# One chain of softmax steps for each chunk of a head pair, instead of one for the two chunks of a head pair

## The chip, the cores and the metric

The kernel runs on one core of a Trainium2 chip. The metric is the device time of one execution in microseconds, as the median of several runs. A profile of one execution goes with it. The engines are named as in the profile: PE is TensorE (PEld its weight loads), DVE is VectorE, ACT is ScalarE, POOL is GpSimd, and SP issues most of the transfers. Each engine works through its own queue in order and waits on semaphores where it needs another engine's result.

## The reference, cut to what matters

The kernel is one step of a hybrid decoder layer, for a prompt of 256 tokens and for 8 sample tokens together (264 columns). One combined input projection gives the operands of a sliding-window attention (16 heads of 64, 4 key heads, window 128, a learned sink per head) and of a state-space mixer; an output projection, a cross-attention and a convolutional feed-forward part follow. The change touches the prompt's sliding-window attention alone:

```python
qb = q.reshape(b, nb, WINDOW, N_KV_HEADS, Q_PER_KV, HEAD_DIM)      # nb = 2 chunks of 128 tokens
logits = jnp.einsum('bnqkgd,bnskd->bnkgqs', qb, kk) * HEAD_DIM ** -0.5
mask = ((diff >= 0) & (diff <= WINDOW))[None] & ((blk > 0) | (sj >= WINDOW)[None])
p = sink_softmax(logits, mask[None, :, None, None], sinks...)       # softmax over the keys and the sink
o = jnp.einsum('bnkgqs,bnskd->bnqkgd', p.astype(v.dtype), vv)
```

Chunk 0 has 128 keys (its own chunk), chunk 1 has 256 (both chunks). The query's RMS norm is not applied to the queries; its factor per row, `rq`, is the scale of the exponential.

## The kernel before, in words

All activations lie with features on the 128 partitions and tokens along the free axis. Weights come in tiles of 128 x 2048 on SP's queue (line 74); ScalarE rounds each half to `whi` (L86, some by VectorE) and VectorE takes the rest `wlo` (L87). Each product is three matmuls (L101 to L103). The input projection goes by pairs of output blocks, `in_pair` (L324): pair 0 gives the keys, pair 1 the values, pairs 2 to 5 the queries, 6 to 9 the B and C operands of the mixer, 10 to 17 its x (two pairs for each `conv_group`), 18 to 25 its gate z. A pair's two results are read out by VectorE at high priority, for the mixer into a ring of three `u` buffers, from which VectorE and ScalarE compute a convolution.

PSUM has eight banks, by tag: `mm` three, `t` two, and `s`, `x` and `y` one each (L58). The pairs write to `mm`, but pair 0 and the odd pairs above 13 write to `t` (L328), so pair 15 is the first behind the attention that needs both `t` banks.

The prompt's attention (`attn_prompt`, L401) runs after the queries' pairs in the text, once for each of eight pairs of heads j, with two chunks c of 128 queries:

1. logits of two heads by one matmul (L410), for chunk 0 into a `t` bank and for chunk 1 into the `s` bank;
2. VectorE adds the mask into a tile in SBUF (L411) and takes the row maxima (L412). The tile of chunk 0 has the tag `e0` (two buffers), that of chunk 1 the tag `h0` (three buffers). The profile calls both `pe`;
3. for both chunks together (128 x 4): times the negative factor `nrq` (L414), the minimum with the negative sink (L415), the sink added (L416), and one exponential for the sink (L417);
4. four exponentials with their row sums (L420); for both chunks together the sink's part added and the reciprocal (L422, L423); four scalings by it (L427);
5. for each chunk: transposes by PE into a `t` bank (L164), a copy to SBUF by ScalarE (L433, tile `pt`), weighted sums of the values by PE into another `t` bank (L437), and a copy to `attn` (L439).

So one head pair takes five `t` tiles: logits, then transposes and sums of chunk 0, then of chunk 1. The statistics tile `st` has four buffers. The sample's attention (`attn_sample`, L457) follows, with two `s` tiles, two `t` tiles (L490 and L497) and two `h0` tiles; the sample's part of the mixer (`ssd_sample`, L644) loads its state on POOL's queue (L651) into `h0` tiles as well.

The order on the engines is not the order of the text. A planner runs the whole program through a simulation at build time, with its own costs, and puts on each engine the earliest written instruction that is ready there (parts under `tc.high_priority()` first). The order that it finds is fixed in the program. Tiles of one tag take turns in its buffers, and what needs a buffer waits until the tile before has been read.

Of the kernel before, what the change touches and what calls it, by code (L numbers as in the profile page):

```python
# [7 lines left out]
F32 = mybir.dt.float32  # L8
F32R = mybir.dt.float32r
AF = mybir.ActivationFunctionType  # L10
ALU = mybir.AluOpType
AX = mybir.AxisListType
# [35 lines left out]
def hybrid_decoder_step_kernel(ctx: ExitStack, tc: tile.TileContext, I, O):  # L48
    nc = tc.nc
    V, S, P, PE = nc.vector, nc.scalar, nc.gpsimd, nc.tensor  # L50
# [9 lines left out]
    def psum(tag):  # L60
        return ps.tile([128, 512], F32, tag=tag, name=tag, bufs=banks[tag])
# [87 lines left out]
    def pc(name, i=0, n=1):  # L149
        o = _PC[name][0]  # L150
        return par[:, o + i:o + i + n]
# [6 lines left out]
    maskb = cst[:, C_MASK:C_MASK + 256]  # L158
# [3 lines left out]
    def tr(out, in_):  # L162
        k = in_.shape[0]
        PE.transpose(out, in_, cst[0:k, C_ID:C_ID + k])  # L164
# [56 lines left out]
    mp = mix.enter_context(tc.tile_pool(name="mp", bufs=1))  # L221
# [7 lines left out]
    p = psum("mm")  # L229
# [41 lines left out]
    p = psum("x")  # L271
# [5 lines left out]
    p = psum("x")  # L277
# [114 lines left out]
    p = psum("y")  # L392
# [5 lines left out]
    nsink = mp.tile([128, 16], F32, name="nsink")  # L398
    V.tensor_scalar(out=nsink, in0=pc("sink_p", 0, 16), scalar1=-1.0, scalar2=None, op0=ALU.mult)

    def attn_prompt(j, rq, nrq):  # L401
        pp = j // 4
        ps_ = [psum("t"), psum("s")]
        evs = [mp.tile([128, 2, 128], F32, tag="e0", name="pe0", bufs=2), mp.tile([128, 2, 256], F32, tag="h0", name="pe", bufs=3)]
        st = mp.tile([128, 3, 2, 2], F32, tag="st", name="st", bufs=4)
        mx, den, es = st[:, 0], st[:, 1], st[:, 2]
        for c in range(2):
            nk = 128 * (c + 1)
            s3 = ps_[c][:, 0:2 * nk].rearrange("p (h k) -> p h k", h=2)
            PE.matmul(s3, qT[:, j, c * 128:c * 128 + 128], kbd[:, pp, :, 0:nk], start=True, stop=True)  # L410
            V.tensor_tensor(out=evs[c], in0=s3, in1=maskb[:, 256 - nk:256].unsqueeze(1).broadcast_to([128, 2, nk]), op=ALU.add)  # L411
            V.tensor_reduce(out=mx[:, c, :], in_=evs[c], op=ALU.max, axis=AX.X)  # L412

        V.tensor_tensor(out=mx, in0=mx, in1=nrq, op=ALU.mult)  # L414
        V.tensor_tensor(out=mx, in0=mx, in1=nsink[:, 2 * j:2 * j + 2].unsqueeze(1).broadcast_to([128, 2, 2]), op=ALU.min)  # L415
        V.tensor_tensor(out=es, in0=mx, in1=pc("sink_p", 2 * j, 2).unsqueeze(1).broadcast_to([128, 2, 2]), op=ALU.add)  # L416
        S.activation(out=es, in_=es, func=AF.Exp)  # L417
        for c in range(2):
            for h in range(2):
                S.activation(out=evs[c][:, h, :], in_=evs[c][:, h, :], func=AF.Exp, scale=rq[:, c, h:h + 1], bias=mx[:, c, h:h + 1],  # L420
                             accum_out=den[:, c, h:h + 1])
        V.tensor_tensor(out=den, in0=den, in1=es, op=ALU.add)  # L422
        V.reciprocal(out=den, in_=den)  # L423
        for c in range(2):
            e, nk, nb = evs[c], 128 * (c + 1), c + 1
            for h in range(2):
                V.tensor_scalar(out=e[:, h, :], in0=e[:, h, :], scalar1=den[:, c, h:h + 1], scalar2=None, op0=ALU.mult)  # L427
            p = psum("t")
            for h in range(2):
                for kb in range(nb):  # L430
                    tr(p[:, (h * nb + kb) * 128:(h * nb + kb) * 128 + 128], e[:, h, kb * 128:kb * 128 + 128])
            pt = mp.tile([128, 4, 128], F32, tag="bc", name="pt", bufs=2)
            S.copy(out=pt[:, 0:2 * nb, :], in_=p[:, 0:2 * nk].rearrange("p (a q) -> p a q", q=128))  # L433
            o = psum("t")
            for h in range(2):
                for kb in range(nb):
                    PE.matmul(o[64 * h:64 * h + 64, 0:128], vn[:, kb, pp, 64 * h:64 * h + 64], pt[:, h * nb + kb, :],  # L437
                              start=kb == 0, stop=kb == nb - 1)
            S.copy(out=attn[:, j, c * 128:c * 128 + 128], in_=o[:, 0:128])  # L439
# [14 lines left out]
    for j in range(8):  # L454
        attn_prompt(j, rqs[:, j], nrqs[:, j])
# [102 lines left out]
    for c in range(2):  # L558
        p = psum("x")
# [4 lines left out]
    for w, XT in enumerate((BT, CT)):  # L564
        p = psum("x")
# [70 lines left out]
    p = psum("x")  # L636
# [143 lines left out]
    p = psum("y")  # L780
# [460 lines left out]
```

## Time and profile before

| | |
|---|---|
| median of 3 runs | 1481.5 us (1478.03 to 1483.37) |
| the profiled execution | 1478.83 us, its span 1477.1 us |
| PE busy | 1423.7 us (96%) |
| DVE busy | 1070.8 us (72%) |
| ACT busy | 788.1 us (53%) |
| the prompt's attention, first logits to last copy | 103.1 to 258.2 us of the span |
| PE clock granted, mean | 0.984 |

In the profile a row of the timeline reads: start, length, engine, line, operation, output <- inputs, shape, count, and in brackets how long the engine stood idle before it and what released it. Lines of a helper stand for all its calls, so L164 is every transpose and L101 to L103 every projection; the tile names tell them apart (`t<-cst,pe` is a transpose of attention weights). Matmuls overlap, so the steps between their starts say more than their lengths.

### The profile page before, as it was taken

To read this page: it belongs to the slowest core of one execution; us is meant where nothing else is said; L and a number is where in the kernel's file an instruction comes from. 1 tells how busy PE (TensorE), PEld (TensorE's weight loads), DVE (VectorE), ACT (ScalarE), POOL (GpSimd) and SP (SyncE) were. 2 spreads that over 40 slices of the span, in tenths; PEclk is the share of its full clock that TensorE was granted. 3 is DMA by queue.
4 is the path that set the end of the run, shared out by engine and by line. 5 is a ranking of instruction groups with operands and counts; after the bars stand their busy time and mean duration, and the time that the engine had idled before them with its cause. 6 is when DMAs were issued, how large, how long until landed. Compare 5 with 4: busy or idle time off the path is not lost.

```text
span 1477.1 us, 28639 instructions
## 1 busy us (share of the span) xinstructions
PE 1423.7 (96%) x11453; PEld 1390.2 (94%) x11453; DVE 1070.8 (72%) x1985; ACT 788.1 (53%) x1308; POOL 190.1 (13%) x366
## 2 busy tenths in 40 slices
PE   6999996999999999989899999999999999999999
PEld 5999995999999999979899999999999999999999
DVE  7747886799985667887999766566666656665664
ACT  5555665367765446566877544445345434543442
POOL 4100000321324111114312000000000100000000
PEclk9999997899999999999999999999999999999999
DMA  6764443577767554884898555555554554555554
GB/s 234 269 196 143 144 150 107 176 250 244 249 215 264 181 191 172 317 333 170 325 340 325 184 187 182 173 192 178 176 193 174 178 194 172 181 191 172 184 201 145
DMA packets 59222, 304.65 MB, mean 206 GB/s; under 512 B 8848, under 2 KB 13904, under 8 KB 29392
## 3 DMA queue, kind: packets, MB, share of 16 engines
q1 hardware_dynamic: 53584, 283.94, 54.9%
q0 software_dynamic: 5504, 18.88, 3.5%
q8 instruction: 90, 1.47, 0.4%
q14 instruction: 44, 0.36, 0.1%
HBM read 287.06 MB, written 16.28 MB: 205 GB/s over the span
## 4 chain that ended last, share of the span: by engine, by line
PE 71%; DVE 11%; DMA 9%; issue 4%; ACT 3%; POOL 1%; SPq 1%; DVEq 0%; ACTq 0%; POOLq 0%
PE mm L102 16%; PE mm L101 16%; PE mm L103 15%; PE t L103 7%; PE t L101 7%; PE t L102 7%; DVE wlo L87 3%; DMA wraw<-in_w_in_dram 2%; DVE hn L1007 1%; DMA wraw<-in_w_out_dram 1%; DMA wraw<-in_w_up_dram 1%; ACT whi L86 1%; DMA hn<-in_h_dram 1%; DMA vt<-in_mvT_dram 1%; PE t L164 1%
## 5 line engine op out<-in xcount | busy, mean ns | idle before, releaser
L87 DVE TENSOR_TENSOR wlo<-wraw,whi 128x1024 fp32r<-128x1024 f32 x448 | 552.6, 1238 | 267.7 <-ACT whi L86 264.1
L86 ACT CAST whi<-wraw 128x1024 fp32r<-128x1024 f32 x444 | 461.1, 1049 | 525.9 <-PE mm L102 301.2
L103 PE MATMUL t<-x2h,wlo 128*128 128x264 f32 x704 | 198.8, 286 | 4.1 <-DVE wlo L87 4.1
L101 PE MATMUL t<-x2h,whi 128*128 128x264 f32 x704 | 200.3, 285 | 1.5 <-ACT whi L86 1.5
L101 PE MATMUL mm<-x2h,whi 128*128 128x264 f32 x704 | 199.4, 284 | 1.0 <-DVE res L975 0.7
L102 PE MATMUL t<-x2l,whi 128*128 128x264 f32 x704 | 199.9, 285 | 0.0
L103 PE MATMUL mm<-x2h,wlo 128*128 128x264 f32 x704 | 197.4, 284 | 2.1 <-DVE wlo L87 2.0
L102 PE MATMUL mm<-x2l,whi 128*128 128x264 f32 x704 | 199.2, 284 | 0.0
L102 PE MATMUL mm<-hl,whi 128*128 128x264 f32 x704 | 198.8, 283 | 0.0
L103 PE MATMUL mm<-hh,wlo 128*128 128x264 f32 x704 | 198.6, 283 | 0.0
L101 PE MATMUL mm<-hh,whi 128*128 128x264 f32 x704 | 196.9, 284 | 0.0
L103 PE MATMUL mm<-xh,wlo 128*128 128x264 f32 x608 | 174.7, 291 | 1.1 <-DVE wlo L87 1.1
L102 PE MATMUL mm<-xl,whi 128*128 128x264 f32 x608 | 174.5, 288 | 0.0
L101 PE MATMUL mm<-xh,whi 128*128 128x264 f32 x608 | 174.3, 288 | 0.0
L103 PEld LDWEIGHTS t<-x2h,wlo 128*128 128x128 f32 x704 | 132.3, 189 | 4.7 <-DVE wlo L87 4.7
L101 PEld LDWEIGHTS t<-x2h,whi 128*128 128x128 f32 x704 | 133.5, 190 | 1.7 <-ACT whi L86 1.7
L103 PEld LDWEIGHTS mm<-x2h,wlo 128*128 128x128 f32 x704 | 131.1, 188 | 3.0 <-DVE wlo L87 3.0
L101 PEld LDWEIGHTS mm<-x2h,whi 128*128 128x128 f32 x704 | 132.4, 188 | 1.4 <-issue 0.8
L102 PEld LDWEIGHTS t<-x2l,whi 128*128 128x128 f32 x704 | 133.5, 190 | 0.0
L102 PEld LDWEIGHTS mm<-x2l,whi 128*128 128x128 f32 x704 | 132.5, 188 | 0.0
L102 PEld LDWEIGHTS mm<-hl,whi 128*128 128x128 f32 x704 | 132.5, 188 | 0.0
L103 PEld LDWEIGHTS mm<-hh,wlo 128*128 128x128 f32 x704 | 132.1, 188 | 0.0
(416 smaller groups left out, 3086.7 us busy)
## 6 DMA issues: line engine op xcount, KB each, us to landing
wraw<-in_w_up_dram SPq DMA_DIRECT2D x88, 1024.0 KB, 4.9
wraw<-in_w_in_dram SPq DMA_DIRECT2D x52, 1024.0 KB, 5.1
wraw<-in_w_dn_dram SPq DMA_DIRECT2D x44, 1024.0 KB, 4.9
wraw<-in_w_out_dram SPq DMA_DIRECT2D x24, 1024.0 KB, 4.9
h<-in_h_dram POOLq DMA_DIRECT2D x32, 256.0 KB, 3.4
hn<-in_h_dram SPq DMA_DIRECT2D x16, 512.0 KB, 7.3
out_state_s_dram<-hn POOLq DMA_DIRECT2D x16, 512.0 KB, 6.2
pb<-dram_p SPq DMA_DIRECT2D x4, 1028.0 KB, 10.0
```

Source lines behind the costliest of these rows:

```text
L86: S.copy(out=hi, in_=x)
L87: V.tensor_tensor(out=lo, in0=x, in1=hi.bitcast(F32), op=ALU.subtract)
L101: PE.matmul(out, wh, xh, start=start, stop=False)
L102: PE.matmul(out, wh, xl, start=False, stop=False)
L103: PE.matmul(out, wl, xh, start=False, stop=stop)
L164: PE.transpose(out, in_, cst[0:k, C_ID:C_ID + k])
L1007: V.scalar_tensor_tensor(out=h[:, b, :], in0=bbs[g][:, b, :], scalar=xds[:, k, b:b + 1], in1=h[:, b, :], op0=ALU.mult, op1=ALU.add)
```

## The change

Each chunk of each head pair gets the whole chain for itself. The logits of both chunks go to the `s` bank, both tiles of masked logits are taken from the tag `h0` (a tile for 256 keys, of which chunk 0 uses the first 128), and the statistics of a chunk are a tile of their own, on two columns. The steps that took both chunks together (L414 to L417, L422, L423) are done for each chunk. Masks, maxima, exponentials, scalings, transposes, copies and sums are the same as before in number and size. The tag `e0` is gone.

```diff
     def attn_prompt(j, rq, nrq):
         pp = j // 4
-        ps_ = [psum("t"), psum("s")]
-        evs = [mp.tile([128, 2, 128], F32, tag="e0", name="pe0", bufs=2), mp.tile([128, 2, 256], F32, tag="h0", name="pe", bufs=3)]
-        st = mp.tile([128, 3, 2, 2], F32, tag="st", name="st", bufs=4)
-        mx, den, es = st[:, 0], st[:, 1], st[:, 2]
         for c in range(2):
             nk = 128 * (c + 1)
-            s3 = ps_[c][:, 0:2 * nk].rearrange("p (h k) -> p h k", h=2)
+            p = psum("s")
+            s3 = p[:, 0:2 * nk].rearrange("p (h k) -> p h k", h=2)
             PE.matmul(s3, qT[:, j, c * 128:c * 128 + 128], kbd[:, pp, :, 0:nk], start=True, stop=True)
-            V.tensor_tensor(out=evs[c], in0=s3, in1=maskb[:, 256 - nk:256].unsqueeze(1).broadcast_to([128, 2, nk]), op=ALU.add)
-            V.tensor_reduce(out=mx[:, c, :], in_=evs[c], op=ALU.max, axis=AX.X)
-
-        V.tensor_tensor(out=mx, in0=mx, in1=nrq, op=ALU.mult)
-        V.tensor_tensor(out=mx, in0=mx, in1=nsink[:, 2 * j:2 * j + 2].unsqueeze(1).broadcast_to([128, 2, 2]), op=ALU.min)
-        V.tensor_tensor(out=es, in0=mx, in1=pc("sink_p", 2 * j, 2).unsqueeze(1).broadcast_to([128, 2, 2]), op=ALU.add)
-        S.activation(out=es, in_=es, func=AF.Exp)
-        for c in range(2):
+            e = mp.tile([128, 2, 256], F32, tag="h0", name="pe", bufs=3)
+            ev = e[:, :, 0:nk]
+            V.tensor_tensor(out=ev, in0=s3, in1=maskb[:, 256 - nk:256].unsqueeze(1).broadcast_to([128, 2, nk]), op=ALU.add)
+            st = mp.tile([128, 8], F32, tag="st", name="st", bufs=4)
+            mx, den, es = st[:, 0:2], st[:, 2:4], st[:, 4:6]
+            V.tensor_reduce(out=mx, in_=ev, op=ALU.max, axis=AX.X)
+
+            V.tensor_tensor(out=mx, in0=mx, in1=nrq[:, c, :], op=ALU.mult)
+            V.tensor_tensor(out=mx, in0=mx, in1=nsink[:, 2 * j:2 * j + 2], op=ALU.min)
+            V.tensor_tensor(out=es, in0=mx, in1=pc("sink_p", 2 * j, 2), op=ALU.add)
+            S.activation(out=es, in_=es, func=AF.Exp)
             for h in range(2):
-                S.activation(out=evs[c][:, h, :], in_=evs[c][:, h, :], func=AF.Exp, scale=rq[:, c, h:h + 1], bias=mx[:, c, h:h + 1],
-                             accum_out=den[:, c, h:h + 1])
-        V.tensor_tensor(out=den, in0=den, in1=es, op=ALU.add)
-        V.reciprocal(out=den, in_=den)
-        for c in range(2):
-            e, nk, nb = evs[c], 128 * (c + 1), c + 1
+                S.activation(out=e[:, h, 0:nk], in_=e[:, h, 0:nk], func=AF.Exp, scale=rq[:, c, h:h + 1], bias=mx[:, h:h + 1],
+                             accum_out=den[:, h:h + 1])
+            V.tensor_tensor(out=den, in0=den, in1=es, op=ALU.add)
+            V.reciprocal(out=den, in_=den)
             for h in range(2):
-                V.tensor_scalar(out=e[:, h, :], in0=e[:, h, :], scalar1=den[:, c, h:h + 1], scalar2=None, op0=ALU.mult)
+                V.tensor_scalar(out=e[:, h, 0:nk], in0=e[:, h, 0:nk], scalar1=den[:, h:h + 1], scalar2=None, op0=ALU.mult)
             p = psum("t")
+            nb = c + 1
```

## The prediction

> **What bounds the kernel now.** I read the page first, then windows around the attention, then the order of TensorE there. The page says that TensorE is the bound over the whole span, and that one stretch is an exception:
>
> ```profile
> span 1477.1 us, 28639 instructions
> PE 1423.7 (96%) x11453; PEld 1390.2 (94%) x11453; DVE 1070.8 (72%) x1985; ACT 788.1 (53%) x1308; POOL 190.1 (13%) x366
> PE   6999996999999999989899999999999999999999
> DVE  7747886799985667887999766566666656665664
> PEclk9999997899999999999999999999999999999999
> ```
>
> Each digit is 36.9 us. The seventh slice of PE (221 to 258 us) is the only one inside the kernel at 6, and the granted clock is down there too. The windows cut that place out (columns: stretch, its length, then busy us and instructions of PE, weight loads, DVE, ACT, POOL, then the clock granted to PE, the DMA share and GB/s):
>
> ```profile
> 103.20:112.00 8.80, 8.80 (x69) 8.27 (x68) 4.75 (x8) 5.42 (x8) 0.00 (x0) 1.00 0.42 149
> 112.00:237.70 125.70, 125.70 (x1014) 117.76 (x1012) 103.13 (x253) 76.47 (x155) 0.73 (x1) 1.00 0.42 144
> 237.70:258.80 21.10, 9.07 (x44) 5.37 (x42) 11.32 (x35) 11.53 (x34) 0.81 (x2) 0.61 0.27 97
> 258.80:266.00 7.20, 7.20 (x35) 7.20 (x35) 4.14 (x6) 0.00 (x0) 1.68 (x4) 0.50 0.30 109
> 266.00:270.00 4.00, 4.00 (x21) 4.00 (x21) 3.17 (x10) 0.00 (x0) 1.81 (x4) 0.54 0.41 122
> 300.00:420.00 120.00, 117.33 (x966) 112.21 (x965) 117.05 (x215) 86.08 (x145) 30.79 (x38) 1.00 0.72 246
> ```
>
> From 112 to 237.7 us TensorE never stops. From 237.7 to 266 it runs out of projection work: 16.3 of 28.3 us busy, at a clock of 0.61 and 0.50. What it does there is the end of the attention, which it meets in its own order:
>
> ```profile
> 240.83 0.43 PE L164 MATMUL t<-cst,pe 128*128 128x128 f32 x2 [2.94 <-DVE pe L427]
> ...
> 247.29 1.22 PE L410 MATMUL t<-kv,attn 128*128 128x256 f32 x2
> 253.06 0.66 PE L164 MATMUL t<-cst,pe 128*128 128x128 f32 x2 [4.55 <-DVE pe L427]
> ...
> 258.74 6.97 PE L497 MATMUL t<-pTs,vc 128*128 128x8 f32 x32 [0.50 <-issue]
> 265.56 0.77 PE L498 MATMUL t<-dgs,cst 128*128 128x128 f32 x2
> 265.99 0.57 PE L101 MATMUL t<-xh,whi 128*128 128x264 f32 x1
> 266.36 0.42 PE L102 MATMUL t<-xl,whi 128*128 128x264 f32 x1
> 266.58 0.42 PE L103 MATMUL t<-xh,wlo 128*128 128x264 f32 x1
> ```
>
> At 265.99 a projection goes on, and it writes into `t`: it is pair 15, the first one behind the attention that takes its two banks from that tag, and all `t` tiles of the attention and of the sample attention stand before it. So the end of the attention, not TensorE's work, sets when pair 15 begins. Why the attention is so late is seen in one head pair in the middle of it (j = 1 and the first step of j = 2):
>
> ```profile
> 131.02 0.70 PE L410 MATMUL t<-kv,attn 128*128 128x256 f32 x2
> 142.48 0.27 PE L164 MATMUL t<-cst,pe 128*128 128x128 f32 x1
> ...
> 145.95 0.44 PE L437 MATMUL t<-pt,vn 128*64 128x128 f32 x4
> 146.32 0.65 PE L164 MATMUL t<-cst,pe 128*128 128x128 f32 x4
> 150.18 0.67 PE L437 MATMUL t<-pt,vn 128*64 128x128 f32 x8
> 150.78 0.70 PE L410 MATMUL t<-kv,attn 128*128 128x256 f32 x2
> ```
>
> The logits of chunk 0 take a `t` bank at 131.02; then come the transposes of chunk 0, its weighted sums, the transposes of chunk 1, its sums, and straight after those (150.78) the next head pair's logits. Five tiles of two banks go round in the written order, and a head pair starts only when the former is through: 19.8 us each. Five such starts lie between this one and 247.29; the mean of the six steps is (247.29 - 131.02) / 6 = 19.4 us.
>
> **The change, part by part.**
>
> *Logits of chunk 0 from `t` to `s`.* The matmuls are the same, so TensorE's work is unchanged. The round of `t` falls from five tiles to four per head pair, and none of them belongs to a later head pair's start. What paces the chunks next? Three candidates. (a) `t`: transposes at 142.48, 146.32 and (by its sums) 150.18 are 3.8 and 3.9 us apart. (b) The three `h0` tiles, which now hold all sixteen chunks instead of eight:
>
> ```profile
> 131.75 0.42 DVE L411 TENSOR_TENSOR pe<-t,cst 128x256 f32<-128x256 f32 x1
> ```
>
> a tile is held from this mask to the transposes at 142.48, about 11 us, so three tiles give one chunk per 3.7 us. (c) The one `s` bank is held from a logits matmul to its mask, 131.02 to 132.2, about 1.2 us. Hence some 4 us per chunk: 16 x 4 = 64 us from 112, and 11 for the first one's latency, so the attention would be over near 187 us. Even at 7 us per chunk it ends at 112 + 11 + 112 = 235, before TensorE gets to pair 15. A chunk's pace can be 1.8 times my estimate before the stall comes back.
>
> *What the stall is worth.* The 16.27 us of TensorE work in it, at the clocks 0.61 and 0.50, are 9.07 x 0.61 + 7.20 x 0.50 = 9.1 us at full clock. They are still to be done, somewhere before pair 15. Pair 15 could then start at 237.7 + 9.1 = 246.8 instead of 266.0: 19.2 us. Its first matmuls follow each other at 0.22 us (266.36, 266.58), while the clock stands at 0.54, against 0.12 just before the stall:
>
> ```profile
> 237.49 0.28 PE L102 MATMUL mm<-xl,whi 128*128 128x264 f32 x1
> 237.61 0.28 PE L103 MATMUL mm<-xh,wlo 128*128 128x264 f32 x1
> ```
>
> Over the 4.00 us to 270.0 that is 4.00 x (1 - 0.54) = 1.8 us. The stall costs 21.0 us. This is the end of the gain's range; the other end is nothing.
>
> *Small operations per chunk.* Five small VectorE steps per head pair become ten (multiply, minimum, add; sum, reciprocal), on 2 columns instead of 4, and ScalarE's exponential of the sink becomes two:
>
> ```profile
> L414 DVE TENSOR_TENSOR st<-st,nrqs x8: 100/153/164, 114.0 to 249.5; 128x4 f32<-128x4 f32 x8
> L416 DVE TENSOR_TENSOR st<-st,par x8: 143/158/164, 114.4 to 249.9; 128x4 f32<-128x4 f32 x8
> L423 DVE RECIPROCAL st<-st x8: 157/172/180, 119.5 to 252.4; 128x4 f32<-128x4 f32 x8
> L417 ACT ACTIVATE st<-st x8: 188/190/199, 118.0 to 251.4; 128x4 f32<-128x4 f32 x8
> ```
>
> 8 x 5 x 0.16 = 6.4 us more on VectorE, 8 x 0.19 = 1.5 us on ScalarE. Masks, maxima, exponentials and scalings stay as they are in number and size, at most on a slice of a larger tile. In one head pair they are, beside the mask above:
>
> ```profile
> 132.21 1.01 DVE L412 TENSOR_REDUCE st<-pe 128x2 f32<-128x256 f32 x2
> ...
> 139.11 1.00 DVE L427 TENSOR_SCALAR pe<-pe,st 128x128 f32<-128x128 f32 x4
> ...
> 147.01 0.69 DVE L411 TENSOR_TENSOR pe<-s,cst 128x512 f32<-128x512 f32 x1 [0.72 <-PE t L164]
> ```
>
> With five small steps of 0.16 that is 0.42 + 0.69 + 1.01 + 1.00 + 0.8 = 3.9 us of VectorE per head pair, 4.7 after the change. ScalarE was busy 76.47 of 125.7 us and hides its 1.5. VectorE was busy 4.75 + 103.13 + 11.32 + 4.14 = 123.3 us from 103.2 to 266; with 6.4 more, and pair 15 at 246.8, it has 129.7 in 143.6 us: 90%. The nearest rows for what that does to TensorE are the second window (82%, no idle time) and the last (97.5%, 2.7 of 120 us idle, 2.2%). At most 2.2% of 143.6 is 3.2 us. But the chunks are now bunched: VectorE's part of them is 8 x 4.7 = 38 us, in 75 us (112 to 187) instead of 146, and what else it does, 82% less the attention's 3.9 in 19.4, thus 62%, asks for another 46 us there: 84 us of work in 75. The surplus of 9 delays convolutions, whose three `u` buffers let TensorE run on for about a pair. I take a third of it as reaching TensorE, 3 us (ends: 0, if the buffers hold, and 9). Crowding together: 6 us, between 0 and 12.
>
> *Queues.* No transfer is added or moved by the text, and no wait is put in front of the weight loads on SP. POOL's queue is touched: its loads of the sample's state take the same `h0` tiles as the chunks and stand behind the last of them.
>
> ```profile
> POOL h L651 <- PE t L164: 78.5, 2, 76.8
> ```
> ```profile
> 258.54 2.86 DMA h<-in_h_dram
> 261.43 0.70 DVE h L652
> ```
>
> The chain of waits goes on through these loads and the products on VectorE after the attention. They come earlier as the tiles do, into a time after 190 us in which the chains are over and VectorE has room. That may lighten the stage from 300 us on; TensorE's idle time there is 2.7 us, so I count it as nothing and let it stretch the lower end by 2.
>
> *Sum*, against the profiled execution (1478.83 us, span 1477.1): 1478.8 - 21.0 + 6 = 1463.8. The median of the runs, 1481.5, is 2.7 above that execution, and so I forecast 1466.5.
>
> **Rivals.**
>
> *B: the stall stays and the added operations come on top.* The chunks go one behind the other instead of three abreast, because VectorE's queue puts other work between the steps of a chain: for j = 1 the mask at 131.75 is followed by transposes 10.7 us later, though VectorE's own steps in it sum to 0.42 + 1.01 + 0.8 + 1.00 = 3.2. It takes 7 us per chunk, as computed, for that to decide, which is a tile held for 21 us; the 10.7 speaks against it. Then 1481.5 + 6.4 = 1488, or 1481.5 if the small steps are hidden as now. [...]
>
> *C: slower, since TensorE waits for each chunk.* TensorE's order is fixed by the planner. Where a chunk's transposes stand in it before VectorE has scaled the chunk, all projections behind them wait. The stall shows that price in the open:
>
> ```profile
> PE t L164 <- DVE pe L427: 7.5, 2, 4.5
> ```
>
> that is 3.75 us a time. Up to 237 us no such wait occurs, with VectorE at 82%; with dense chains it would be near 100%. The point that decides is 21.0 / 16 = 1.3 us per chunk. At 2 us the cost is 32: 1481.5 + 11 = 1492.5. If the clock fell as in the stall (0.61 with waits of 2.94 to 4.55 us) for the 75 us, another 29 us would come on top. [...]
>
> *D: half the stall goes*, with crowding at its upper end: 1481.5 - 10.5 + 6 to 12, 1477 to 1483.
>
> **How the numbers follow.** My forecast A (stall gone, crowding 0 to 12: 1460.5 to 1472.5) gets 0.58, for the pace has a reserve of 1.8. C gets 0.20, B 0.14, D 0.08. A measurement of this kernel tells about 0.3% from no change, 4.4 us: faster means under 1477. A gives faster; D is half faster, half same; B is same in a quarter of its cases; C is slower. So 0.62 faster, 0.08 same, 0.30 slower. The range reaches from A's lower end less those 2, 1458, to C at 1493; beyond it I leave a deeper C and the rest of A's bounds.
>
> **What would show it.** The seventh slice of PE at 9 and its clock at 9; pair 15's first matmul near 250 us; logits all into `s`, the last of them before 190 us; VectorE in the bunched part above 90%; 40 more small VectorE steps of about 0.16 us. The forecast is wrong if transposes make PE wait in many of the sixteen chunks, if the last chunk still ends after 240 us, or if what is gained at 266 us is lost again between 300 and 420, where VectorE is at 97.5% and hands nothing back.

## The result, and the profile after

The changed kernel takes 1458.5 us (median of 6 runs, 1454.73 to 1460.13), against 1478.5 us for the kernel before (median of 6, 1477.09 to 1483.37). The ratio is 0.9855, with a 95% interval of 0.9837 to 0.9874: 20.0 us less by the medians, 21 by the ratio. The forecast was 15.0 us less on the profiled execution. The median lies half a microsecond inside the range, at its very end; the ratio puts the time at 0.9855 x 1478.5 = 1457.1, just below it.

The page of the profile of the changed kernel, with the same lines as shown of before:

```profile
span 1453.0 us, 28695 instructions
PE 1415.6 (97%) x11453; PEld 1386.2 (95%) x11453; DVE 1068.6 (74%) x2025; ACT 787.9 (54%) x1316; POOL 191.4 (13%) x366
PE   6999999999999999989899999999999999999999
DVE  7748878999966667779998665667566656665664
PEclk9999999999999999999999999999999999999999
```

The 6 in the seventh slice of PE is gone, and so are the 7 and 8 of the clock there. VectorE has 40 instructions more, as it should, and ScalarE 8. The windows of the same stretches (columns as before: stretch, length, busy us and instructions of PE, weight loads, DVE, ACT, POOL, then granted clock, DMA share, GB/s):

```profile
112.00:187.00 75.00, 75.00 (x582) 66.62 (x581) 67.51 (x220) 53.88 (x138) 0.73 (x1) 1.00 0.38 131
187.00:237.70 50.70, 50.70 (x403) 49.78 (x403) 38.03 (x87) 20.80 (x37) 6.96 (x13) 0.93 0.51 173
237.70:266.00 28.30, 27.16 (x232) 25.87 (x231) 27.35 (x53) 16.46 (x28) 2.68 (x5) 1.00 0.67 224
```

Between 237.7 and 266 us TensorE now works 27.16 of 28.30 us at full clock. From 112 to 187, where nearly all of the sixteen chains' work on VectorE lies, VectorE is at 67.51 / 75 = 90% and TensorE still has no idle time. TensorE's order shows where the attention went (the timeline of PE; start and length in us):

```profile
124.96 0.44 PE L436 MATMUL t<-pt,vn 128*64 128x128 f32 x4
199.68 0.66 PE L436 MATMUL t<-pt,vn 128*64 128x128 f32 x8
211.24 4.45 PE L496 MATMUL t<-pTs,vc 128*128 128x8 f32 x32
243.64 0.63 PE L164 MATMUL x<-cst,xs 128*128 128x128 f32 x4 [1.15 <-DVE xw L602]
250.40 0.28 PE L101 MATMUL t<-xh,whi 128*128 128x264 f32 x1
```

The first row is the weighted sums of the first chunk, the second those of the last: fifteen steps in 199.68 - 124.96 = 74.7 us, 5.0 us per chunk. The sample's sums stand at 211 us, where they stood at 258.74 before. Pair 15, the first projection behind the attention that takes `t`, starts at 250.40 and not at 265.99: 15.6 us earlier. The row at 243.64, a transpose of the mixer that waits 1.15 us for VectorE, is TensorE's only wait between 112 us and pair 15.

What it did not get is in the windows just behind the sample's sums:

```profile
211.20:216.00 4.80, 4.80 (x37) 4.80 (x35) 4.76 (x8) 1.03 (x2) 0.54 (x1) 0.78 0.49 174
216.00:220.00 4.00, 4.00 (x20) 4.00 (x20) 2.48 (x10) 0.00 (x0) 1.59 (x3) 0.50 0.90 324
220.00:224.00 4.00, 4.00 (x33) 4.00 (x32) 2.67 (x5) 2.23 (x3) 1.07 (x2) 0.92 0.50 153
```

TensorE is never idle there, and its clock falls to 0.50 all the same. That costs 4.80 x 0.22 + 4.00 x 0.50 + 4.00 x 0.08 = 3.4 us; over 187 to 237.7 us it is 50.7 x (1 - 0.93) = 3.5.

What was won behind pair 15 is found by windows that run from pair 15 to the output projection of the attention, whose first matmul reads `ath`. Before:

```profile
270.00:300.00 30.00, 28.52 (x237) 26.50 (x237) 26.53 (x46) 13.25 (x22) 7.91 (x12) 1.00 0.64 212
300.00:425.00 125.00, 122.33 (x1004) 116.81 (x1003) 122.05 (x223) 89.82 (x151) 33.95 (x40) 1.00 0.70 240
```
```profile
424.96 0.28 PE L101 MATMUL mm<-ath,whi 128*128 128x264 f32 x1
```

After:

```profile
250.40:270.00 19.60, 19.60 (x165) 18.81 (x164) 19.60 (x40) 12.35 (x24) 2.68 (x5) 1.00 0.78 249
270.00:300.00 30.00, 30.00 (x252) 29.21 (x251) 30.00 (x57) 16.97 (x33) 7.14 (x8) 1.00 0.69 242
300.00:405.70 105.70, 103.50 (x842) 97.32 (x841) 102.31 (x192) 80.64 (x134) 28.11 (x32) 1.00 0.68 231
```
```profile
405.71 0.28 PE L101 MATMUL mm<-ath,whi 128*128 128x264 f32 x1
```

At `ath` the changed kernel is 425.0 - 405.7 = 19.3 us ahead. Of these, 15.6 are pair 15's earlier start. 1.8 are the recovering clock behind the stall (4.00 us at 0.54 before, none after). The rest is idle time of TensorE: 1.48 + 2.67 = 4.15 us before, 2.20 after, so 1.9. The two profiled executions differ by 24.1 us in the end, the medians by 20.0: the last 4 us, behind `ath`, where the two texts are the same, are not in the medians (the profiled execution of the changed kernel was its shortest), and nothing is read from them. The 1.9 us come from one execution of each kernel as well, and the six executions of the changed kernel lie 5.4 us apart, so a difference of that size isn't clear of noise.

### The profile page after: what moved, and what is told of

It is laid out like the page before. It is cut to its first block, busy times and chain, and to the rows that moved or that the text cites. A ratio compares the mean times of both kernels' runs of the same rounds, so it can differ in the third digit from the quotient of the medians.

```text
span 1453.0 us, 28695 instructions
## 1 busy us (share of the span) xinstructions
PE 1415.6 (97%) x11453; PEld 1386.2 (95%) x11453; DVE 1068.6 (74%) x2025; ACT 787.9 (54%) x1316; POOL 191.4 (13%) x366
## 4 chain that ended last, share of the span: by engine, by line
PE 74%; DVE 14%; DMA 5%; issue 3%; ACT 3%; POOL 1%; SPq 0%; ACTq 0%; DVEq 0%; POOLq 0%
PE mm L101 16%; PE mm L102 16%; PE mm L103 16%; PE t L103 7%; PE t L101 7%; PE t L102 7%; DVE wlo L87 4%; DMA wraw<-in_w_in_dram 2%; DMA wraw<-in_w_ck_dram 1%; DMA wraw<-in_w_out_dram 1%; DVE h L651 1%; ACT whi L86 1%; POOL accm L179 1%; PE s L407 1%; DVE hn L1006 1%
## 5 line engine op out<-in xcount | busy, mean ns | idle before, releaser
L86 ACT CAST whi<-wraw 128x1024 fp32r<-128x1024 f32 x444 | 461.3, 1049 | 528.5 <-PE mm L102 302.0
L87 DVE TENSOR_TENSOR wlo<-wraw,whi 128x1024 fp32r<-128x1024 f32 x448 | 551.8, 1236 | 260.7 <-ACT whi L86 255.1
```

The source lines that it names most:

```text
L86: S.copy(out=hi, in_=x)
L87: V.tensor_tensor(out=lo, in0=x, in1=hi.bitcast(F32), op=ALU.subtract)
```

## Experiments

Every kernel was timed beside the kernel before, whose median was then 1479.2 us (for e1 to e4), 1477.7 us (e5 to e8) or 1480.8 us (e9 to e11); the ratios, and the differences worked out from them, are to those. The first three take the change apart, the next two test the two sizes that came out otherwise than forecast, and the others ask where the gain behind pair 15 comes from.

**1. The bank alone (e1_merged_s).** The kernel before, with the logits of chunk 0 moved to `s`; the small steps still take both chunks together.

```diff
-        ps_ = [psum("t"), psum("s")]
...
-            s3 = ps_[c][:, 0:2 * nk].rearrange("p (h k) -> p h k", h=2)
+            s3 = psum("s")[:, 0:2 * nk].rearrange("p (h k) -> p h k", h=2)
```

> The kernel before with one edit: both chunks' logits go to the s bank; the chain of statistics stays common to the two chunks, and chunk 0's tile stays in e0. Theory T (the five t tiles per head pair make one head pair wait for the last): the last weighted sums come before 215 us instead of 257, pair 15 starts near 248 to 252, and the time is 1455 to 1465 against 1478.5 before. Rival R (what helped is that each chunk has a chain of its own): nothing moves, pair 15 near 266 and 1475 to 1482.

Measured: 1461.8 us (1461.44 to 1465.01), ratio 0.989 (0.9874 to 0.9905), so 16.3 us less than before. Pair 15 in the timeline of PE:

```profile
249.86 0.28 PE L101 MATMUL t<-xh,whi 128*128 128x264 f32 x1
```

That is as early as with the whole change. The five `t` tiles per head pair were what tied the head pairs together; the separate chains aren't needed for it.

**2. The chains alone (e2_chains_t).** The changed kernel, with the logits of chunk 0 back in `t`.

```diff
-            p = psum("s")
+            p = psum("s" if c else "t")
```

> The changed kernel with one edit back: chunk 0's logits go to a t bank again; sixteen chains and the h0 tiles stay. Theory T: the stall comes back, the last weighted sums after 235 us, time 1472 to 1488. Rival R (chains of their own): no stall, 1456 to 1463 as with the whole change.

Measured: 1475.8 us (1472.39 to 1480.32), ratio 0.998 (0.9966 to 0.9994), 3 us less than before. The stall is back, as the timeline and the window show:

```profile
260.86 0.57 PE L101 MATMUL t<-xh,whi 128*128 128x264 f32 x1
```
```profile
237.70:266.00 28.30, 22.69 (x142) 19.81 (x141) 18.38 (x62) 12.21 (x33) 2.85 (x6) 0.68 0.29 99
```

TensorE is busy 22.69 of 28.30 us at a clock of 0.68. The separate chains shorten a head pair a little (pair 15 comes 5.1 us earlier than before) but cannot undo the tie. The two parts nearly add up by the ratios: 16.3 + 3.0 = 19.3 us, against 21 for both.

**3. The stall taken away without touching the attention (e3_pair15_mm).** The kernel before, with pair 15 writing to `mm`, so that pair 17 is the first one to need `t`.

```diff
-        proj([w_in[2 * i], w_in[2 * i + 1]] if i else pre, A, evac, tag="t" if not i or (i > 13 and i % 2) else "mm")
+        proj([w_in[2 * i], w_in[2 * i + 1]] if i else pre, A, evac, tag="t" if not i or (i > 15 and i % 2) else "mm")
```

> The kernel before with one edit: pair 15 writes to the mm banks instead of t (pair 17 is now the first behind the attention that needs both t banks). The attention stays as late as it is, near 250 us. If the price of its lateness is pair 15's wait for t, TensorE goes on through that time and the time falls to 1457 to 1466. If the price is elsewhere (the loads of the sample's state behind the h0 tiles, VectorE's work after the attention), it stays at 1473 to 1480.

Measured: 1472.5 us (1470.22 to 1473.73), ratio 0.9955 (0.994 to 0.997), 6.7 us less than before and between the two forecasts: the stall goes from its place, but most of its price does not.

```profile
237.70:266.00 28.30, 26.61 (x221) 25.72 (x219) 24.13 (x61) 20.84 (x46) 0.00 (x0) 1.00 0.52 183
266.00:300.00 34.00, 29.98 (x194) 27.61 (x195) 22.43 (x45) 9.26 (x20) 7.36 (x14) 0.75 0.48 149
```

The old place of the stall is filled, at full clock, so pair 15's need of `t` was what stopped TensorE there. But the attention is no faster, and the loss moves on by one pair: 266 to 300 us stands at 29.98 of 34 us and a clock of 0.75, and the last sums of the attention and those of the sample now stand in it:

```profile
269.64 1.13 PE L437 MATMUL t<-pt,vn 128*64 128x128 f32 x8 [0.67 <-ACT pt L433]
...
271.67 6.97 PE L497 MATMUL t<-pTs,vc 128*128 128x8 f32 x32 [0.50 <-ACT xs L530]
```

Going round a late chain moves the wait; the chain itself has to be shorter.

**4. More small steps (e4_small_ops).** The changed kernel, with the addition of the sink (L417) done six times over: 16 x 5 = 80 more VectorE steps, twice what the change added. In the changed kernel one such group reads (mean ns between the lowest and the highest, then first and last start):

```profile
L417 DVE TENSOR_TENSOR st<-st,par x16: 149/153/161, 113.1 to 186.0; 128x2 f32<-128x2 f32 x16
```
```diff
-            V.tensor_tensor(out=es, in0=mx, in1=pc("sink_p", 2 * j, 2), op=ALU.add)
+            for _ in range(6):
+                V.tensor_tensor(out=es, in0=mx, in1=pc("sink_p", 2 * j, 2), op=ALU.add)
```

> The changed kernel with the addition of the sink (line 417 there) done six times in each chunk instead of once: 80 more VectorE steps of 0.155 us, 12.4 us in the stretch from 112 to 200 us, nothing else. If VectorE has room there (as the reading of the result says), the time stays within 3 us of 1458.5. If crowding has the price that the prediction gave it, 6 us or more for such an addition, it is 1464 to 1472.

Measured: 1461.4 us (1452.6 to 1464.73), ratio 0.9862 (0.9829 to 0.9896), not to be told from the changed kernel's 0.9855. The interval is some 5 us to either side, so the time alone doesn't exclude a cost of a few microseconds; the trace says more.

```profile
112.00:187.00 75.00, 75.00 (x585) 68.00 (x584) 69.18 (x251) 52.43 (x123) 0.73 (x1) 1.00 0.43 145
```

80 x 0.153 = 12 us of further VectorE work in the chains leave TensorE without a gap: 75.00 of 75 us, with VectorE at 92%. The chains only end later (last sums at 221 us instead of 200), which is still before anything needs them. TensorE has no idle time up to 250 us either, and pair 15 starts at 248.6, 1.8 us earlier than in the changed kernel: up to there the added steps cost nothing.

**5. Wider sums of the sample (e5_wide_sums).** In the changed kernel the 32 matmuls of the sample's weighted sums read 8 columns each. Here each reads 32 (its own 8, and 24 that are not used), the padding being zeroed; the product behind them (L497) moves to an `s` tile of its own for want of room. The 8 columns that are used are the same.

```diff
-        pT = mp.tile([128, 128], F32, tag="bc", name="pTs", bufs=2)
+        pT = mp.tile([128, 152], F32, tag="bc", name="pTs", bufs=2)
+        V.memset(pT[:, 128:152], 0.0)
...
-            PE.matmul(o[:, 8 * i:8 * i + 8], vc[:, i, :], pT[:, 8 * i:8 * i + 8], start=True, stop=True)
-        PE.matmul(o[:, 128:256], hm, dg, start=True, stop=True)
+            PE.matmul(o[:, 32 * i:32 * i + 32], vc[:, i, :], pT[:, 8 * i:8 * i + 32], start=True, stop=True)
+        o2 = psum("s")
+        PE.matmul(o2[:, 0:128], hm, dg, start=True, stop=True)
```

> The changed kernel with the sample's sums (32 matmuls of 8 columns) widened to 32 columns each, of which 8 are used; the rest of the sample's attention unchanged. Theory K (the clock falls behind these because they stream too little, not because PE stands idle): the 32 matmuls take about as long as now, some 4.5 us, the clock stays at 1.00 behind them, and pair 15 starts 3 us earlier; the time falls by 0 to 3.5 us, to 1455 to 1458.5. Rival: 32 columns are still too few, or the clock falls for another reason, and the windows behind them show 0.5 again.

Measured: 1468.7 us (1464.69 to 1470.11), ratio 0.9923 (0.9894 to 0.9951), slower than the change.

```profile
187.00:237.70 50.70, 50.70 (x418) 49.61 (x418) 41.79 (x98) 25.57 (x42) 6.98 (x13) 0.97 0.55 188
216.00:220.00 4.00, 4.00 (x22) 4.00 (x22) 3.93 (x11) 0.00 (x0) 1.61 (x3) 0.57 0.87 290
340.00:380.00 40.00, 34.06 (x256) 31.05 (x255) 29.47 (x58) 32.05 (x52) 10.59 (x14) 0.96 0.53 174
```

The dip of the clock becomes smaller, 50.7 x 0.03 = 1.5 us instead of 3.5, and pair 15 comes 1.7 us earlier. But behind the sums the clock still falls, to 0.57. Nor is the smaller dip the work of the columns: e11_state_held, whose sums read 8 columns as in the changed kernel, has the same one (its 32 matmuls start between 212.6 and 215.9 us; from 211.2 to 216 us its clock is 1.00, and from 187 to 237.7 us 0.97):

```profile
216.00:220.00 4.00, 4.00 (x22) 4.00 (x22) 1.38 (x7) 0.00 (x0) 0.54 (x1) 0.57 0.71 293
```

So the run doesn't show that the narrowness of the sums plays a part, and what makes the clock fall remains open. The time is lost elsewhere: at 340 to 380 us TensorE idles for 5.9 us, most of it in one wait for a weight tile that ScalarE rounds (L86):

```profile
345.88 0.51 PE L101 MATMUL mm<-xh,whi 128*128 128x264 f32 x1 [3.68 <-ACT whi L86]
```

ScalarE is busy 32.05 of the 40 us there, and 32.46 in the changed kernel. Why this edit should bring such a wait isn't plain from its text, and the next runs take that up.

**6 and 8. Edits of next to nothing (e6_one_more, e8_merged_s_more).** The addition of the sink is done twice, in the changed kernel (16 more steps, 2.4 us) and in e1_merged_s (8 more). All that such an edit can do beside that is to make the planner deal the order anew.

```diff
-            V.tensor_tensor(out=es, in0=mx, in1=pc("sink_p", 2 * j, 2), op=ALU.add)
+            for _ in range(2):
+                V.tensor_tensor(out=es, in0=mx, in1=pc("sink_p", 2 * j, 2), op=ALU.add)
```

> The changed kernel with the addition of the sink done twice in each chunk: 16 more VectorE steps, 2.5 us, a work that costs next to nothing, but enough to make the planner deal the whole order anew. If the time of a version hangs on its own order after the attention (theory O), it lies somewhere between 1455 and 1464, not tied to the 2.5 us. If the order does not matter, it is within 1 us of the changed kernel's 1458.5.

> The merged chain with all logits in s (e1), with the addition of the sink done twice in each head pair: 8 more VectorE steps, 1.3 us, and a new order by the planner. If what parts e1 (1461.8) from the changed kernel (1458.5) is the order that the planner happened on, this lies anywhere between 1456 and 1465. If it is the common chain that costs 3 us, it is 1461 to 1464.

Measured: 1463.2 us (1457.87 to 1469.26), ratio 0.989 (0.9845 to 0.9934), and 1465.7 us (1462.14 to 1469.45), ratio 0.9911 (0.9882 to 0.9941). Both medians are some 4 us above that of the kernel that they were made from, with intervals that overlap its own; e6 lies in its first forecast, e8 just above both of its own. In the profiled executions TensorE's idle time is in the stage behind pair 15. These are the windows from 300 to 440 us, of the kernel before:

```profile
300.00:440.00 140.00, 137.33 (x1128) 131.81 (x1127) 136.32 (x249) 97.73 (x165) 36.99 (x42) 1.00 0.70 239
```

of the changed kernel:

```profile
300.00:440.00 140.00, 137.59 (x1118) 130.79 (x1117) 125.29 (x229) 96.39 (x159) 33.09 (x36) 1.00 0.71 247
```

of e1_merged_s, e4_small_ops, e6_one_more and e8_merged_s_more, in this order:

```profile
300.00:440.00 140.00, 132.62 (x1066) 126.12 (x1065) 121.91 (x222) 90.43 (x151) 33.50 (x37) 0.99 0.69 237
```
```profile
300.00:440.00 140.00, 134.93 (x1083) 128.94 (x1082) 123.32 (x223) 90.17 (x148) 33.74 (x38) 0.98 0.70 235
```
```profile
300.00:440.00 140.00, 134.38 (x1097) 128.21 (x1096) 123.40 (x224) 95.22 (x160) 31.28 (x35) 1.00 0.69 240
```
```profile
300.00:440.00 140.00, 133.66 (x1083) 128.08 (x1081) 120.57 (x221) 90.93 (x152) 32.96 (x35) 0.99 0.70 237
```

All four start pair 15 within 2 us of the changed kernel, and lose 5.1 to 7.4 us of TensorE's time here, where the changed kernel loses 2.4 and the kernel before 2.7. VectorE is less busy in them, not more. What ends the waits differs: in e4 it is ScalarE's rounding (L86) for 4.8 of the 5.1 us, in e1 the waits are spread over five results of VectorE and ScalarE. The window also reaches past `ath`, and up to there e6 goes as well as the changed kernel: 155.8 us from pair 15 to `ath` against 155.3, where e8 takes 158.9, e4 160.1 and e1 162.4. Of e6's idle time 2.1 us lie between 420 and 440 us.

So with pair 15 at 250 us the rest can go well or less well. That the dealt order decides which is argued here, not shown: an order is fixed in its program, and yet the executions of e4 lie between 1452.6 and 1464.73 us and those of e6 between 1457.87 and 1469.26, 12 and 11 us apart, which is more than the medians of these kernels differ. The profiles, too, are of single executions, that of the changed kernel its shortest and that of e4 its longest.

**7, 9 and 10. Is it VectorE's work on the sample's state?** In the changed kernel the loads of that state and the products on them (L651) begin before pair 15, since the `h0` tiles come free earlier. e7_h0_four gives the tag `h0` a fourth buffer; e9_pool_products gives the product of the changed kernel to POOL; e10_four_pool does both. The edit of e7, at each of the four tiles of that tag, and that of e9:

```diff
-            e = mp.tile([128, 2, 256], F32, tag="h0", name="pe", bufs=3)
+            e = mp.tile([128, 2, 256], F32, tag="h0", name="pe", bufs=4)
```
```diff
-                V.tensor_tensor(out=h0, in0=h0, in1=cb, op=ALU.mult)
+                P.tensor_tensor(out=h0, in0=h0, in1=cb, op=ALU.mult)
```

> The changed kernel with four h0 tiles instead of three, for the chunks and for the sample's state alike. If the three tiles pace the chunks (5.0 us each as measured), the chunks come at 4 us or less and the attention ends near 185 us instead of 200; the time stays within 3 us of 1458.5, since pair 15 is not what waits any more. If the two t banks or VectorE pace them, the pace stays at 5 us.

> The changed kernel with the 32 products of the sample's state (0.68 us each on VectorE) done by POOL instead: 22 us less on VectorE, most of it in the stretch from 250 to 400 us where VectorE is busy without a gap. Theory V (after the attention VectorE's load and its order set how well TensorE is kept busy): PE's idle time from 250 to 430 falls from some 3.5 us to under 2 and the time is 1450 to 1458. Rival: VectorE does not bound there, or POOL's queue holds up its own loads, and the time is 1458 to 1470.

> The version with four h0 tiles (1472), whose extra 14 us come after the attention, with the products of the sample's state on POOL as well. Theory V (four tiles let the state's work on VectorE crowd together between 190 and 320 us): with 22 us taken off VectorE the time falls by 8 us or more, to 1455 to 1464. Rival (the loss comes from somewhere else in the new order): 1468 to 1476.

Measured: 1472.3 us (1468.83 to 1480.11), ratio 0.9956 (0.9935 to 0.9977); 1475.9 us (1472.36 to 1479.97), ratio 0.9971 (0.9954 to 0.9987); 1476.4 us (1471.15 to 1480.05), ratio 0.9974 (0.9954 to 0.9994). All three lose most of the gain. For e7 the forecast of its time (within 3 us of 1458.5) fails, e9 lies above both of its ranges, and e10 0.4 us above its rival's.

e7 settles what paces the chunks: with four tiles instead of three the last sums come at 197.9 us against 199.7, still 5.0 us per chunk, so it isn't the `h0` tiles; whether it is the two `t` banks, the one `s` bank or VectorE, no run tells. Pair 15 starts at 246.5, earlier than in the changed kernel, so what e7 loses it loses behind that. It also does more work on the state early. The windows of tile `h` alone (DVE, POOL) from 187 to 250 us, of the changed kernel and then of e7:

```profile
187.00:250.00 63.00, 14.04 (x21) 6.97 (x13) 0.95 0.52 179
```
```profile
187.00:250.00 63.00, 21.60 (x33) 10.72 (x20) 0.97 0.67 224
```

and of e7 again, all engines:

```profile
300.00:340.00 40.00, 33.80 (x256) 30.66 (x255) 40.00 (x85) 25.38 (x47) 6.71 (x7) 0.91 0.53 183
```

VectorE is full and TensorE waits 6.2 of 40 us, where the changed kernel, with VectorE just as full, waits 1.4. State work done in a lump would explain it, but this window holds little more of it: tile `h` takes 8.42 us of VectorE's time here and 7.47 in the changed kernel. So that cause isn't shown. If it were right, taking the work off VectorE should help, and e9 did not get faster:

```profile
300.00:340.00 40.00, 35.77 (x299) 33.88 (x298) 39.38 (x63) 25.37 (x47) 21.58 (x21) 1.00 0.70 239
```

VectorE is nearly as full as in the changed kernel (39.38 us, 40.00 there) with 63 instructions instead of the changed kernel's 81. The groups of VectorE's instructions by shape in this window say why (busy us and mean ns of one behind the bar). The changed kernel:

```profile
L87 DVE TENSOR_TENSOR wlo<-wraw,whi 128x1024 fp32r<-128x1024 f32 x11 | 13.3, 1215 | 0.0
L528 DVE SCALAR_TENSOR_TENSOR c<-u,par,c 128x256 f32<-128x256 f32 x11 | 5.8, 530 | 0.0
L652 DVE TENSOR_REDUCE ych<-h 128x4 f32<-128x512 f32 x5 | 3.4, 675 | 0.0
L660 DVE TENSOR_TENSOR xds<-ysam,dsb 128x32 f32<-128x32 f32 x1 | 0.2, 184 | 0.0
```

and with the products on POOL:

```profile
L87 DVE TENSOR_TENSOR wlo<-wraw,whi 128x1024 fp32r<-128x1024 f32 x11 | 15.4, 1409 | 0.4 <-ACT whi L86 0.4
L528 DVE SCALAR_TENSOR_TENSOR c<-u,par,c 128x256 f32<-128x256 f32 x12 | 8.8, 738 | 0.0
L652 DVE TENSOR_REDUCE ych<-h 128x4 f32<-128x512 f32 x8 | 5.3, 674 | 0.0
L660 DVE TENSOR_TENSOR xds<-ysam,dsb 128x32 f32<-128x32 f32 x1 | 1.3, 1262 | 0.0
```

Three of these groups are longer in e9, where POOL is busy 21.58 of the 40 us (7.18 in the changed kernel): L528 went from 530 to 738 ns, L87 from 1215 to 1409 and the one L660 from 184 to 1262, while the reduction L652 stayed at 675. Others kept their length too (L682 412 and 416 ns, L593 677 and 682), and what parts the two kinds isn't shown. The product itself is also longer on POOL; over the whole span the group reads, for the changed kernel and for e9:

```profile
L651 DVE TENSOR_TENSOR h<-h,cb 128x512 f32<-128x512 f32 x32 | 21.5, 685 | 2.9 <-DMA cb<-dram_bc 1.7 <-DMA h<-in_h_dram 1.1
```
```profile
L651 POOL TENSOR_TENSOR h<-h,cb 128x512 f32<-128x512 f32 x32 | 48.6, 1530 | 32.2 <-DMA h<-in_h_dram 18.4 <-DMA cb<-dram_bc 13.7
```

Of VectorE's groups by shape over the span, 90 hold the same instructions in both kernels, 1915 of them; they sum to 1122.0 us in the changed kernel and to 1145.7 in e9: 23.7 us more, against the 21.5 that the products take on VectorE. In e10 VectorE is busy 299.8 us from 112 to 460 us, 4.8 less than the 304.6 of the changed kernel. So e9 did not take the load off VectorE and e10 little of it, and they don't tell whether less load would help. In e9 pair 15 also comes at 255.2, 4.8 us later.

**11. The early state work held back (e11_state_held).** The changed kernel, with a small copy on VectorE, ahead of the sample's mixer part, into the tile that POOL's first load of `cb` needs. The copy reads a result of pair 15, so none of that work can begin before pair 15 is through.

```diff
+    hold = mp.tile([128, 4, 128], F32, tag="cb", name="hold", bufs=1)
+    V.tensor_copy(out=hold[:, 0, 0:8], in_=xs[2][:, 2, 0:8])
```

> The changed kernel, with the sample's state held back: its first tile on POOL's queue must wait for a small copy of a result of pair 15, so no product runs before about 262 us, as in the kernel before. Pair 15 itself stays near 250. Theory Q (the part of the gain that comes after pair 15 is VectorE work of the state done ahead of it, 14 us): the stretch from pair 15 to the output projection is longer than the changed kernel's 155.3 us by 3 or more, and the time is 1462 to 1468. Rival (that part is only the planner's luck with the order): no tie, 1454 to 1462.

Measured: 1455.4 us (1452.81 to 1458.5), ratio 0.9835 (0.9812 to 0.9859). The window of tile `h` (DVE, POOL), and pair 15:

```profile
187.00:250.00 63.00, 0.00 (x0) 1.81 (x3) 0.97 0.43 144
```
```profile
249.65 0.28 PE L101 MATMUL t<-xh,whi 128*128 128x264 f32 x1
```

None of the products is done early, and nothing is lost, as the rival said: the gain doesn't rest on state work done ahead. This is the shortest time of all, though its interval overlaps that of the changed kernel, so that it can't be called faster than that one.

## Why the prediction was right and where it was off

- **The bound and the mechanism held.** The end of the attention set pair 15's start (e3: with pair 15 off `t`, the stall goes from its place), and chunk 0's logits in `t` made the attention late (e1 and e2: without them pair 15 starts at 249.9, with them at 260.9).
- **The stall, -21.0: measured -17.4.** The 1.8 for the recovering clock came as computed. Of the 19.2 for pair 15, 15.6 came: 250.40 instead of 246.8. I had costed the work of the stall at full clock once it was moved. But before, the 32 matmuls of the sample's sums took 6.97 us at the low clock inside the stall, and in the changed kernel they take 4.45 us and the clock falls behind them: a loss of 3.5 us that the stall had hidden did not go with it. With the wait of 1.15 us at 243.64 that makes 4.65, some 1 us more than the 3.6 that are missing; this rest is not traced. The dip isn't fixed either: in e11, with the same matmuls, it costs 1.7 us (4.00 x 0.43).
- **Crowding, +6 (0 to 12): this term failed.** Up to pair 15 it was next to nothing: TensorE 75.00 of 75 us with VectorE at 90%, one wait of 1.15 us for VectorE at 243.64 (it is in the 15.6 already), and with e4's 80 further steps no idle time up to 250 us. Its 3.2 us were read off another stage, where VectorE at 97.5% goes with 2.2% idle time of TensorE; a share of busy time did not carry over from that stage to this one. Its other 3 us were a surplus of work that I sent on to TensorE through the `u` buffers; instead VectorE's work there came to 67.51 of 75 us, not 84, as the chains took longer, which nobody waited for. Behind pair 15, where the forecast saw no change but a possible loss, TensorE idled 1.9 us less than before in the profiled executions. With -17.4 in place of -21.0 and -1.9 in place of +6 the sum is -19.3, and the medians differ by 20.0.
- **The pace, 4 us per chunk: measured 5.0**, the last sums at 199.7 against the 187 forecast for the attention's end. The pace had room up to 7 us by my sum, so the miss cost nothing. Candidate (b), the three `h0` tiles, falls with e7; between the others nothing decides.
- **Queues, nothing.** The state's loads and products did come earlier, as said (21 products and reductions before 250 us); e11, without them, is no slower.
- **"The gained time is lost between 300 and 420, where VectorE hands nothing back".** This is what I named as a way to be wrong. It did not happen in the changed kernel (2.4 us idle in 300 to 440 against 2.7 before), but it does happen in part in e1, e4, e6 and e8 (5.1 to 7.4). The fear was of the right place, but VectorE's share does not tell the cases apart: it is lower in these four than in the changed kernel.
- **The +2.7 for the median.** The median of three runs stood above the profiled execution; the median of six is 1478.5, below it. Of the 8.0 us by which 1466.5 is too high, 3.0 are this; of the other 5.0 the terms above give 4.3, and 0.7 is left between the profiles and the medians.
- **The rivals.** B (stall stays) and D (half of it) fall with pair 15 at 250.4. The number of VectorE's operations did not bind up to pair 15, where e4's 80 more steps left no gap. Nor is it the breaking up of the steps that brought the gain, as e1 has 16.3 us of it with nothing broken up. C (TensorE waits for each chunk) falls with the idle-free 112 to 187 us. Its 1492.5 reckons a wait of 2 us in each chunk at full clock, and no run shows that. What the runs show of the clock is that it fell to 0.50 with TensorE busy in all 4.00 of 4.00 us (216 to 220), behind 4.45 us of matmuls of 8 columns, and to 0.57 in e5 with four times the columns just as in e11 with 8. Why it fell stays open.

What is not settled: why the changed kernel and e11 come out 3 to 8 us shorter by the medians than e1, e4 and e6, with pair 15 at nearly the same place. The dealt order is one candidate, mere spread between executions another. Early state work is not the cause (e11); what could test a load of VectorE would be a kernel with that load truly gone, and there was none. Nor is it known what e5, e7, e9 and e10 lose 10 to 18 us by, beyond the single waits shown.

## What to carry to other kernels

Count how many tiles of a small ring one step of a chain takes, and whether one of them belongs to the next step's start: moving that one tile to another bank untied the chains and brought 16 of the 20 us, while the rewriting of the small steps brought about 3. Going round the late chain (e3) only moves the wait, and extra small steps on an engine at 90% left no gap on TensorE as long as nobody needed their results earlier. After any edit under a planner, hold a neutral sibling beside it, and several executions of each, before a few microseconds are read as the edit's own: here the medians of siblings that differ in 8 to 80 steps of 0.15 us lay 3 to 5 us apart, and executions of one and the same kernel up to 12.

## What the runs showed of the hardware

- In the changed kernel the clock of TensorE fell to half without an idle gap. In three successive windows of 4 to 4.8 us from 211.2 to 224 us, the first of which holds 32 matmuls of 128 x 8 in 4.45 us, it was 0.78, 0.50 and 0.92, with TensorE busy throughout: 3.4 us lost. The same matmuls in e11 (starts from 212.6 to 215.9 us) were followed by one window at 0.57, 1.7 us lost, and so were matmuls of 32 columns each in e5.
- The products of 128 x 512 in fp32 took POOL 1.53 us each in the mean (e9), against 0.685 on VectorE in the changed kernel. From 300 to 340 us, with POOL busy 21.58 us in e9 and 7.18 in the changed kernel, two groups of VectorE's instructions were longer by 16% (L87) and 39% (L528) in the mean, and a short one (L660) took 1.26 us instead of 0.18; others kept their length. Moving the 32 products to POOL made the kernel 17 us slower, 1475.9 against 1458.5.
